# A decoder layer on one Trainium2 core: full-depth low K products and two gate projections moved ahead of waits

## The chip, the cores and the metric

The kernel runs on one core of one Trainium2 chip. The metric is device time in microseconds from start to end of one execution; lower is better. An execution that is profiled leaves a trace of each engine: PE (TensorE, matmuls) and PEld (its weight loads), DVE (VectorE), ACT (ScalarE), POOL (GpSimd), and the queue of SP (SyncE), which here issues nearly all DMA transfers.

## The reference, cut to what matters

One decoder layer in float32 over 1024 tokens of width 1024:

```python
u = x * (1.0 + scale_m) + shift_m
proj = u @ w_in                      # qa ka va | qb kb vb | ga gb
oa = sliding-window attention of 16 query heads on 2 K/V heads, with sinks
ob = dilated attention, 24 heads in 3 groups (dilation 1, 4, 16), merged by softmax of their log-sums
merged = sigmoid(ga) * (oa @ w_branch_a) + sigmoid(gb) * (ob @ w_branch_b)
x = layer_norm(ALPHA * x + (1.0 + gate_m) * (merged @ w_o))
u = x * (1.0 + scale_f) + shift_f
x = layer_norm(ALPHA * x + (1.0 + gate_f) * swiglu(u))
```

The products must have nearly float32 accuracy. TensorE multiplies values of a shorter format (`fp32r`), so each operand is kept as a high part (the rounded value, made by ACT) and a low part (the rest, made by a subtraction on DVE), and one product is three matmuls: high x high, high x low, low x high.

## The kernel before, in words

**First phase: projections and attention.** `w_in` is cut into 128-column chunks, in the order in which the attention uses them. One chunk is projected by `project`, which goes through `gemm_u`: 48 matmuls of 128x128 on 128x512 (two halves of the tokens, eight slices of the depth, three matmuls each), in 8 steps of 6. Work is grouped in 20 *units*. A B unit (12 of them, `p` pair of heads, `g` dilation group) needs three chunks, in the order K, V, Q; the first A unit needs Q, V, K, and the seven other A units only Q, as they share K and V. `stream` is a generator that yields after each of the 8 steps of each chunk, unit by unit. The first unit's three chunks and one chunk of gates are projected in the prologue (`early`), while the modulated input is still being made, so they yield nothing. Behind the last unit `stream` projects two more gate chunks, `tail_gates` (4 and 5 of `ga`), and stores them to the DRAM tile `ga_d`; the prologue's gate chunk (`early_gate_dc`, 3) is stored there too.

A loop over the units, in four quarters each (`subs`), issues the attention in turns with the stream: `scores` (PE), `turn_probs` of the quarter before (transposes on PE), `exponentials` (ACT), `weigh` of two quarters before (PE), and between them `pump`, which advances the stream to a given number of steps. `lengths` and `ends` hold how many steps belong to each unit; `LEAD` = 6 keeps the stream 6 steps ahead of the scores. Before the first scores the stream is pumped to `ends[0] + LEAD + 2` steps. `soon` and `tick` put off a function by a number of steps: the splitting of K and Q (`k_stacks`, `q_stacks`) is issued two or three steps after a chunk's end, somewhat later for the prologue's.

A unit has two heads, each of depth 64, on the lower (`LO`) and upper (`HI`) 64 partitions. `q_stacks` makes a tile of 128 partitions for each head: the high part of Q on the head's own half, the low part on the other half. `k_stacks` makes `kh`, with the high part of K on both halves (own half by ACT, line 448, other half by ACT again, line 449). So one matmul of depth 128 gives (Q high + Q low) x K high. The low part `kl` is made by DVE (line 454) on the own half; in a B unit both heads share one `kl` tile. The second product (line 501), Q high x K low, has a depth of 64: `LO` for one head, `HI` for the other. One call of `scores` issues four matmuls of depth 128 (line 495) and four of depth 64 (line 501).

**Second phase: branches.** The attention output is read back from DRAM (`oa_d`, `ob_d`), split into `o_hl` tiles by `o_parts` (lines 802, 117 and 118), and multiplied by the branch weights in 24 steps ("w" in `order`: three sets of 8 column chunks). Set 0 (first half of the A branch) has no gate of its own; in sets 1 and 2 each step's result is added up by DVE and multiplied by a gate tile `gt` (`merge`). The gates are in `order` as "g" entries, one ahead of each step of sets 1 and 2, but that of the first step of set 1 (gate 8) stands ahead of step 0. `make_gate` computes a gate with `gemm_u` or, for the indices in `made_early` (8 + the chunk's number), loads it from `ga_d`. `ada` is a generator of side work (the conditioning vectors), of which `make_gate` and the steps each take some.

The last attention outputs are finished while the second phase begins: the last pair's sums go to DRAM and back on POOL's queue, POOL scales the tile `o` and stores it to `oa_d` (lines 604, 609, 618, 619). Memory of the first phase's pool (`att`) is reused by the second phase's pools; a tile of the new pool waits for the last use of the old one at the same place. So where a tile of `att` lies decides what a tile of the second phase waits for.

**Weights.** `Weights` holds a list of pieces of 512 columns, in the order in which they are taken. Three raw tiles (`w_raw`) are loaded ahead on SP's queue; `step` splits the next piece (ACT line 78, DVE line 79) into one of four `w_hi`/`w_lo` pairs. Two steps of each projection and one of each branch step call it. All engines work off their instructions in the order in which the program issues them.

The second half of the kernel (`w_o`, the norm, the SwiGLU layer) is not touched.

Of the kernel before, what the change touches and what calls it, by code (L numbers as in the profile page):

```python
# [10 lines left out]
F32 = mybir.dt.float32  # L11
F32R = mybir.dt.float32r
I32 = mybir.dt.int32
AF = mybir.ActivationFunctionType
OP = mybir.AluOpType
# [3 lines left out]
P = 128  # L19
T = 1024  # L20
# [4 lines left out]
TH = T // 2  # L25
# [73 lines left out]
def decoder_layer(ctx: ExitStack, tc: tile.TileContext, I, out, dbg=None):  # L99
    nc = tc.nc  # L100
# [40 lines left out]

    ws = Weights(nc, wpool)
    EARLY = 3
    early_gate_dc = 3

    def add_chunk(src, pieces, kh, scale=None, dest=None):
        for i in range(pieces):
            ws.add(src[:, i * 512:(i + 1) * 512], kh, scale, dest)

    tail_gates = (4, 5)  # L150
    for e in range(EARLY, 46):
        add_chunk(I["w_in"][e], 2, 4)
    for dc in tail_gates:
        add_chunk(I["w_in"][46 + dc], 2, 4)
# [1 line left out]
    gate_of = {8 + dc: 46 + dc for dc in range(KC)}  # L156
    gate_of.update({16 + dc: 54 + dc for dc in range(KC)})
    branch_w = [I["w_branch_a"][0], I["w_branch_a"][1], I["w_branch_b"]]
    made_early = [8 + dc for dc in (early_gate_dc, *tail_gates)]
    order = []  # L160
    for i in range(len(steps)):
        g = 8 if i == 0 else i + 1
        if g in gate_of and i != 7:
            order.append(("g", g))
        order.append(("w", i))
    for kind, i in order:
        if kind == "g" and i not in made_early:
            add_chunk(I["w_in"][gate_of[i]], 2, 4)
        elif kind == "w":
            b, dc = steps[i]  # L170
            add_chunk(branch_w[b][dc], 1, 4)
# [268 lines left out]

        return rotary(e, r, then)

    def k_stacks(e, r, both, box):

        def stack(res, h):
            own, other = ((LO, HI), (HI, LO))[h]
            kh = att.tile([P, T], F32R, name="kh", bufs=4)
            nc.scalar.activation(kh[own], res[own], AF.Copy)
            nc.scalar.activation(kh[other], res[own], AF.Copy)
            box.setdefault("kh", []).append(kh)  # L450
            los = box.setdefault("kl", [])
            if both or not los:
                los.append(att.tile([P, T], F32R, name="kl", bufs=2))
            nc.vector.tensor_tensor(los[-1][own], res[own], kh[own], op=OP.subtract)  # L454
            if both:
                nc.vector.tensor_tensor(los[-1][other], res[own], kh[own], op=OP.subtract)
            elif h:
                los.append(los[0])

        def then(res):  # L460
            for h in range(2):
                soon(2 + h + (2 if e < EARLY else 0), lambda h=h: stack(res, h))

        return rotary(e, r, then)
# [20 lines left out]
    def scores(un, qr):  # L485

        box, prev, st = un["box"], un["prev"], un["st"]
        probs = att.tile([P, 2, 2, 2, P], F32, name="probs", bufs=2)
        un["probs", qr] = probs
        khs, kls = (box["kh"], box["kl"]) if "kv" not in un else ([kv_a["kh"][un["kv"]]] * 2, [kv_a["kl"][un["kv"]]] * 2)  # L490
        pss = [ps_s.tile([P, 2, 2, P], F32, name="s") for _ in range(2)]
        blocks = [(i, 2 * qr + i, 0 if prev(2 * qr + i) else 1) for i in range(2)]
        for i, b, lo in blocks:
            for h in range(2):
                nc.tensor.matmul(pss[h][:, i, lo:], box["q"][h][:, b * P:(b + 1) * P],  # L495
                                 khs[h][:, (b - 1 + lo) * P:(b + 1) * P], start=i == 0, stop=False,
                                 skip_group_check=True)

        for i, b, lo in blocks:
            for h, own in enumerate((LO, HI)):  # L500
                nc.tensor.matmul(pss[h][:, i, lo:], box["q"][h][own, b * P:(b + 1) * P],  # L501
                                 kls[h][own, (b - 1 + lo) * P:(b + 1) * P], start=False, stop=i == 1,
                                 skip_group_check=True)
        mx = att.tile([P, 2, 2], F32, name="mx", bufs=3)
        for h in range(2):
            for i, b, lo in blocks:
                nc.vector.tensor_tensor_reduce(  # L507
                    out=probs[:, h, i, lo:], in0=pss[h][:, i, lo:], in1=un["mask"][:, lo:], scale=QS, scalar=NEG,
                    op0=OP.add, op1=OP.max, accum_out=mx[:, h, i:i + 1])
            sl = slice(2 * qr, 2 * qr + 2)  # L510
            if "kv" in un:
                nc.vector.tensor_scalar(st[:, 0, h, sl], mx[:, h], un["sink"](h), -1.0, op0=OP.max, op1=OP.mult)  # L512
            else:
                nc.vector.tensor_scalar(st[:, 0, h, sl], mx[:, h], -1.0, None, op0=OP.mult)
# [159 lines left out]
    def sigmoid_half(dst, ps):  # L674
        nc.scalar.activation(dst, ps, AF.Tanh, scale=0.5)
        nc.vector.tensor_scalar(dst, dst, 0.5, 0.5, op0=OP.mult, op1=OP.add)

    def stream():
        for un in units:
            if "b" in un:  # L680
                p, g = un["b"]
                base, r = (p * 3 + g) * 3, B_DIL[g]
                yield from k_stacks(base, r, False, un["box"])
                yield from values(base + 1, r, un["box"])
                yield from q_stacks(base + 2, r, un["box"])
            else:
                yield from q_stacks(36 + un["a"] + 2 * (un["a"] > 0), 1, un["box"])
                if un["a"] == 0:
                    yield from values(37, 1, kv_a)
                    yield from k_stacks(38, 1, True, kv_a)  # L690
        for dc in tail_gates:
            g = att.tile([P, T], F32, name="r", bufs=1)
            yield from project(46 + dc, lambda t, ps: sigmoid_half(g[:, t * TH:(t + 1) * TH], ps))
            nc.sync.dma_start(ga_d[dc], g)

    lengths = [0 if n == 0 else 24 if "b" in un else 24 if un["a"] == 0 else 8 for n, un in enumerate(units)]
    ends = np.cumsum(lengths)
    total = ends[-1] + 8 * len(tail_gates)
    flow = stream()
# [37 lines left out]
    g_early = att.tile([P, T], F32, name="cst", bufs=1)  # L737
    for t, ps in enumerate(gate_banks):
        half = slice(t * TH, (t + 1) * TH)
        nc.scalar.activation(g_early[:, half], ps, AF.Tanh, scale=0.5)  # L740
        nc.scalar.activation(g_early[:, half], g_early[:, half], AF.Copy, bias=0.5, scale=0.5)
    nc.sync.dma_start(ga_d[early_gate_dc], g_early)
    pump(ends[0] + LEAD + 2)
    for s in range(len(subs) + 2):
# [104 lines left out]
    ada = ada_steps()  # L849
    gts = {}  # L850

    def make_gate(i, *steps):
        g = mix.tile([P, T], F32, name="gt", bufs=2)
        gts[i] = g
        if i in made_early:
            nc.sync.dma_start(g, ga_d[i - 8])
            return
        ps = [ps_2.tile([P, TH], F32, name="p2") for _ in range(2)]
        for n, t in enumerate(gemm_u(ps, ws.take(2), *steps)):
            if n % 4 == 2:  # L860
                next(ada, None)
            if t is not None:
                sigmoid_half(g[:, t * TH:(t + 1) * TH], ps[t])

    def merge(b, dc, t, ps, g):
        m = mrg(dc, t)
# [18 lines left out]
                    nc.sync.dma_start(dbg["mg"][dc * P:(dc + 1) * P, t * TH:(t + 1) * TH], mrg(dc, t))  # L885

    for kind, i in order:
        if kind == "g":
            if i in (8, 9, 17):
                ws.prepare(4)  # L890
# [328 lines left out]
    n = 0  # L1219
# [194 lines left out]
```

## Time and profile before

| | |
|---|---|
| median of 3 runs | 1885.06 us (1883.31 to 1887.6) |
| the profiled execution | 1886.68 us, of which its span 1884.6 us |
| mean granted clock of TensorE | 0.992 |
| PE busy | 1827.5 us, 8924 matmuls |
| DVE / ACT / POOL busy | 1154.8 / 784.0 / 600.0 us |
| bytes moved by DMA | 171.85 MB, mean 91 GB/s |

A row of the trace in order of time has the start in us from the span's start, the duration, engine, line, operation, output and inputs, the shapes, how many such instructions follow each other (x4), and in brackets how long the engine was idle before it and what ended that. Matmuls are pipelined: the next one starts before the one before has ended, so the distance of two starts tells what a matmul costs, not its duration. A row for a stretch ("A:B") gives its length, then the busy time of PE, PEld, DVE, ACT and POOL with their instructions, the granted clock, the share of time that the DMA engines were busy, and GB/s.

### The profile page before, as it was taken

Reading aid. Unit: us, or ns where it says so; the run is one execution under the profiler, and the core shown is the slowest. Engines: PE = TensorE matmul, PEld = TensorE weight load, DVE = VectorE, ACT = ScalarE, POOL = GpSimd, SP = SyncE. Lnnn points to the kernel's source line nnn. Section 1 sums busy time; section 2 is a strip of 40 time slices with the busy share of each in tenths; the row PEclk is TensorE's granted clock in tenths of the full one; section 3 lists DMA queues with packets and bytes.
Section 4 is the critical chain, followed back from the end, with each engine's and each line's share of the span. In section 5 each row is a group of like instructions: output and inputs, shape, how many; then the busy total and the mean of one; then the engine's idle time right before and its main releaser. Section 6 shows DMA issues by size and latency. Waiting matters only on the chain.

```text
span 1884.6 us, 24305 instructions
## 1 busy us (share of the span) xinstructions
PE 1827.5 (97%) x8924; PEld 1475.4 (78%) x8924; DVE 1154.8 (61%) x2136; ACT 784.0 (42%) x1664; POOL 600.0 (32%) x389
## 2 busy tenths in 40 slices
PE   6899999999999999989999999999999999999998
PEld 3678887877878767768888878878888888888886
DVE  5865567667667887643645365575565444674567
ACT  3544454544454667743112132653433333421122
POOL 2422323223223312100312242455664333531223
PEclk9999999999999999999999999999999999999999
DMA  8211112112111132144543223122222222442222
GB/s 280 91 34 35 35 36 79 40 39 76 42 57 63 41 95 76 57 168 155 208 137 137 79 72 134 57 90 101 85 78 85 89 79 89 151 134 71 97 84 89
DMA packets 72408, 171.85 MB, mean 91 GB/s; under 512 B 13089, under 2 KB 14177, under 8 KB 72290
## 3 DMA queue, kind: packets, MB, share of 16 engines
q1 hardware_dynamic: 71954, 169.26, 26.3%
q8 instruction: 70, 1.15, 0.3%
q0 software_dynamic: 336, 1.06, 0.2%
q14 instruction: 48, 0.39, 0.1%
HBM read 146.33 MB, written 23.95 MB: 90 GB/s over the span
## 4 chain that ended last, share of the span: by engine, by line
PE 81%; DVE 9%; ACT 4%; issue 3%; POOL 2%; DMA 1%; DVEq 0%; SPq 0%; POOLq 0%; ACTq 0%
PE pf L1108 22%; PE pj L137 7%; PE pj L139 7%; PE pj L138 6%; PE p L138 5%; PE p L139 5%; PE p L137 5%; PE pf L138 5%; PE pf L139 5%; PE pf L137 5%; PE pt L544 2%; PE po L567 2%; PE s L495 1%; PE s L501 1%; DVE probs L507 1%
## 5 line engine op out<-in xcount | busy, mean ns | idle before, releaser
L137 PE MATMUL pj<-u,w_hi 128*128 128x512 f32 x720 | 301.1, 418 | 0.0
L139 PE MATMUL pj<-u,w_lo 128*128 128x512 f32 x720 | 283.7, 394 | 0.0
L138 PE MATMUL pj<-u,w_hi 128*128 128x512 f32 x720 | 282.5, 392 | 0.0
L419 POOL TENSOR_TENSOR rb<-rb,sin_t 128x512 f32<-128x512 f32 x64 | 86.7, 1355 | 502.5 <-DVE rb L417 438.0
L118 DVE TENSOR_TENSOR w_lo<-r,w_hi 128x512 fp32r<-128x512 f32 x110 | 116.2, 1059 | 138.8 <-ACT w_hi L117 137.8
L79 DVE TENSOR_TENSOR w_lo<-w_raw,w_hi 128x512 fp32r<-128x512 f32 x148 | 131.2, 890 | 85.2 <-ACT w_hi L78 83.0
L522 ACT ACTIVATE probs<-probs,st 128x128 f32<-128x128 f32 (+1 forms) x320 | 146.0, 460 | 59.3 <-DVE st L512 30.1
L137 PEld LDWEIGHTS pj<-u,w_hi 128*128 128x128 f32 x720 | 136.2, 189 | 33.4 <-issue 4.7
L139 PEld LDWEIGHTS pj<-u,w_lo 128*128 128x128 f32 x720 | 135.8, 189 | 30.4
L138 PEld LDWEIGHTS pj<-u,w_hi 128*128 128x128 f32 x720 | 136.5, 190 | 22.4
L138 PE MATMUL pf<-wd,h 128*128 128x512 f32 x352 | 137.1, 389 | 0.0
L139 PE MATMUL pf<-wd,h 128*128 128x512 f32 x352 | 137.1, 389 | 0.0
L137 PE MATMUL pf<-wd,h 128*128 128x512 f32 x352 | 137.1, 389 | 0.0
L62 POOL TENSOR_TENSOR w_raw<-w_raw,gate 128x512 f32<-128x512 f32 x60 | 85.5, 1439 | 143.9 <-DMA w_raw<-in_w_down 120.6
L1327 DVE SCALAR_TENSOR_TENSOR zt<-zt,pf 128x512 f32<-128x512 f32 x112 | 75.3, 685 | 79.7 <-PE pf L139 79.7
L420 POOL TENSOR_TENSOR r<-ra,rb 128x512 f32<-128x512 f32 x63 | 114.5, 1817 | 6.1 <-DVE kl L454 1.3
L78 ACT ACTIVATE w_hi<-w_raw 128x512 fp32r<-128x512 f32 x148 | 90.8, 624 | 33.9 <-PE p L138 16.8
L546 ACT ACTIVATE ptsb<-pt 128x512 f32<-128x512 f32 (+1 forms) x128 | 63.5, 547 | 93.4 <-PE pt L544 93.0
L137 PE MATMUL p<-o_hl,w_hi 128*128 128x512 f32 x192 | 76.1, 396 | 6.8 <-ACT o_hl L117 6.8
L137 PE MATMUL p<-u,w_hi 128*128 128x512 f32 x208 | 82.2, 395 | 0.0
L139 PE MATMUL p<-u,w_lo 128*128 128x512 f32 x208 | 81.1, 390 | 0.0
L138 PE MATMUL p<-u,w_hi 128*128 128x512 f32 x208 | 81.0, 389 | 0.0
(305 smaller groups left out, 4266.8 us busy)
## 6 DMA issues: line engine op xcount, KB each, us to landing
w_raw<-in_w_in SPq DMA_DIRECT2D x116, 256.0 KB
r<-in_w_gate_up SPq DMA_DIRECT2D x47, 512.0 KB
a_raw<-in_w_ada SPq DMA_DIRECT2D x32, 512.0 KB
w_raw<-in_w_down SPq DMA_DIRECT2D x44, 256.0 KB
h_raw<-h_d SPq DMA_DIRECT2D x22, 512.0 KB
h_d<-g SPq DMA_DIRECT2D x40, 256.0 KB
wa<-in_w_ada_m SPq DMA_DIRECT2D x16, 512.0 KB
wb<-wt_d SPq DMA_DIRECT2D x24, 256.0 KB
```

The lines of the kernel that those rows point to most:

```text
L62: self.nc.gpsimd.tensor_tensor(self.raws[i], self.raws[i], scale(), op=OP.mult)
L78: self.nc.scalar.activation(hi, raw, AF.Copy)
L79: self.nc.vector.tensor_tensor(lo, raw, hi, op=OP.subtract)
L118: nc.vector.tensor_tensor(lo, src, hi, op=OP.subtract)
L137: nc.tensor.matmul(ps, w[0], m[0], start=first, stop=False)
L138: nc.tensor.matmul(ps, w[0], m[1], start=False, stop=False)
L139: nc.tensor.matmul(ps, w[1], m[0], start=False, stop=last)
L419: eng.tensor_tensor(b, b, sin_t[:, s], op=OP.mult)
L420: eng.tensor_tensor(residue_half(res, r, t), by_residue(a, r), by_residue(b, r), op=OP.add)
L522: nc.scalar.activation(pr, pr, AF.Exp, bias=st[:, 0, h, b:b + 1], accum_out=st[:, 1, h, b:b + 1])
L1108: nc.tensor.matmul(ps, w[:, c], m[:, k], start=first and k == 0 and n == 0, stop=k == 3 and n == 2, skip_group_check=True)
L1327: nc.vector.scalar_tensor_tensor(z, z, ALPHA if gi == 0 else 1.0, pd, op0=OP.mult, op1=OP.add)
```

## The change

Three things change.

1. *K stacks and scores.* The copy of K's high part to the other half is no longer made by ACT but by a DMA on SP's queue, inside the chip's memory. Each head has a `kl` tile of its own, with the low part on the own half (DVE) and copied to the other half by a second DMA. `kl` has four buffers of 4 KB in a partition instead of two. In `scores` the low product uses the whole Q tile and both halves of `kl`, so all eight matmuls have a depth of 128, and it now also holds Q low x K low. The two products of one block and head follow each other.
2. *A lead gate.* Chunk 6 of `ga` is projected in `stream` behind unit 0's chunks (which yield nothing), so ahead of unit 1's K chunk, and stored to `ga_d`. Its 8 steps count as unit 0's length, and the pump before the first scores runs to 16 steps instead of 8. Both operations of its sigmoid run on ACT (`act_sigmoid`). Its tile is a `wb` tile, which thereby gets its place in the pool earlier than before. In the second phase gate 14 is loaded.
3. *A bridge.* Gate 10 (chunk 2 of `ga`) is computed ahead of step 0, behind gate 8, and stored to `ga_d` (`kept=True`); it takes no side work from `ada`. At its own place in set 1 it is loaded.

The lists of weight pieces follow the new order.

```diff
-    early_gate_dc = 3
+    early_gate_dc, lead_gate_dc = 3, 6
...
-    for e in range(EARLY, 46):
+    for e in (46 + lead_gate_dc, *range(EARLY, 46)):
         add_chunk(I["w_in"][e], 2, 4)
...
-    made_early = [8 + dc for dc in (early_gate_dc, *tail_gates)]
+    made_early = [8 + dc for dc in (early_gate_dc, lead_gate_dc, *tail_gates)]
+    bridge = 10
...
+        if i == 0:
+            order.append(("b", bridge))
         order.append(("w", i))
     for kind, i in order:
-        if kind == "g" and i not in made_early:
+        if kind == "b" or (kind == "g" and i not in (*made_early, bridge)):
             add_chunk(I["w_in"][gate_of[i]], 2, 4)
...
-    def k_stacks(e, r, both, box):
+    def k_stacks(e, r, box):
         def stack(res, h):
             own, other = ((LO, HI), (HI, LO))[h]
             kh = att.tile([P, T], F32R, name="kh", bufs=4)
+            kl = att.tile([P, T], F32R, name="kl", bufs=4)
             nc.scalar.activation(kh[own], res[own], AF.Copy)
-            nc.scalar.activation(kh[other], res[own], AF.Copy)
+            nc.sync.dma_start(kh[other].bitcast(F32), kh[own].bitcast(F32))
+            nc.vector.tensor_tensor(kl[own], res[own], kh[own], op=OP.subtract)
+            nc.sync.dma_start(kl[other].bitcast(F32), kl[own].bitcast(F32))
             box.setdefault("kh", []).append(kh)
-            los = box.setdefault("kl", [])
-            if both or not los:
-                los.append(att.tile([P, T], F32R, name="kl", bufs=2))
-            nc.vector.tensor_tensor(los[-1][own], res[own], kh[own], op=OP.subtract)
-            if both:
-                nc.vector.tensor_tensor(los[-1][other], res[own], kh[own], op=OP.subtract)
-            elif h:
-                los.append(los[0])
+            box.setdefault("kl", []).append(kl)
...
             for h in range(2):
-                nc.tensor.matmul(pss[h][:, i, lo:], box["q"][h][:, b * P:(b + 1) * P],
-                                 khs[h][:, (b - 1 + lo) * P:(b + 1) * P], start=i == 0, stop=False,
-                                 skip_group_check=True)
-
-        for i, b, lo in blocks:
-            for h, own in enumerate((LO, HI)):
-                nc.tensor.matmul(pss[h][:, i, lo:], box["q"][h][own, b * P:(b + 1) * P],
-                                 kls[h][own, (b - 1 + lo) * P:(b + 1) * P], start=False, stop=i == 1,
-                                 skip_group_check=True)
+                for n, ks in enumerate((khs, kls)):
+                    nc.tensor.matmul(pss[h][:, i, lo:], box["q"][h][:, b * P:(b + 1) * P],
+                                     ks[h][:, (b - 1 + lo) * P:(b + 1) * P], start=i == 0 and n == 0,
+                                     stop=i == 1 and n == 1, skip_group_check=True)
...
+    def act_sigmoid(dst, ps):
+        nc.scalar.activation(dst, ps, AF.Tanh, scale=0.5)
+        nc.scalar.activation(dst, dst, AF.Copy, bias=0.5, scale=0.5)
...
+            if n == 0:
+                g = att.tile([P, T], F32, name="wb", bufs=1)
+                yield from project(46 + lead_gate_dc, lambda t, ps: act_sigmoid(g[:, t * TH:(t + 1) * TH], ps))
+                nc.sync.dma_start(ga_d[lead_gate_dc], g)
...
-    lengths = [0 if n == 0 else 24 if "b" in un else 24 if un["a"] == 0 else 8 for n, un in enumerate(units)]
+    lengths = [8 if n == 0 else 24 if "b" in un else 24 if un["a"] == 0 else 8 for n, un in enumerate(units)]
...
-    def make_gate(i, *steps):
+    def make_gate(i, *steps, kept=False):
         g = mix.tile([P, T], F32, name="gt", bufs=2)
         gts[i] = g
-        if i in made_early:
+        if i in (*made_early, bridge) and not kept:
             nc.sync.dma_start(g, ga_d[i - 8])
             return
         ps = [ps_2.tile([P, TH], F32, name="p2") for _ in range(2)]
         for n, t in enumerate(gemm_u(ps, ws.take(2), *steps)):
-            if n % 4 == 2:
+            if n % 4 == 2 and not kept:
                 next(ada, None)
...
+        if kept:
+            nc.sync.dma_start(ga_d[i - 8], g)
...
     for kind, i in order:
+        if kind == "b":
+            make_gate(i, kept=True)
+            continue
```

More of the change, by code (lines that the diff above doesn't have):

```diff
@@ L676, in sigmoid_half @@
         nc.vector.tensor_scalar(dst, dst, 0.5, 0.5, op0=OP.mult, op1=OP.add)
+    def act_sigmoid(dst, ps):
+        nc.scalar.activation(dst, ps, AF.Tanh, scale=0.5)
+        nc.scalar.activation(dst, dst, AF.Copy, bias=0.5, scale=0.5)
     def stream():
-        for un in units:
+        for n, un in enumerate(units):
             if "b" in un:
@@ L682, in stream @@
                 base, r = (p * 3 + g) * 3, B_DIL[g]
-                yield from k_stacks(base, r, False, un["box"])
+                yield from k_stacks(base, r, un["box"])
                 yield from values(base + 1, r, un["box"])
@@ L689, in stream @@
                     yield from values(37, 1, kv_a)
-                    yield from k_stacks(38, 1, True, kv_a)
+                    yield from k_stacks(38, 1, kv_a)
+            if n == 0:
+                g = att.tile([P, T], F32, name="wb", bufs=1)
+                yield from project(46 + lead_gate_dc, lambda t, ps: act_sigmoid(g[:, t * TH:(t + 1) * TH], ps))
+                nc.sync.dma_start(ga_d[lead_gate_dc], g)
         for dc in tail_gates:
@@ L739, in decoder_layer @@
         half = slice(t * TH, (t + 1) * TH)
-        nc.scalar.activation(g_early[:, half], ps, AF.Tanh, scale=0.5)
-        nc.scalar.activation(g_early[:, half], g_early[:, half], AF.Copy, bias=0.5, scale=0.5)
+        act_sigmoid(g_early[:, half], ps)
     nc.sync.dma_start(ga_d[early_gate_dc], g_early)
```

## The prediction

> **What bounds the kernel now.** I read the page first (busy shares, chain), then the waits of TensorE, then its order of time around each long wait. The page has PE busy nearly throughout, and the chain that sets the end is mostly PE:
>
> ```profile
> PE 1827.5 (97%) x8924; PEld 1475.4 (78%) x8924; DVE 1154.8 (61%) x2136; ACT 784.0 (42%) x1664; POOL 600.0 (32%) x389
> ...
> PE 81%; DVE 9%; ACT 4%; issue 3%; POOL 2%; DMA 1%; DVEq 0%; SPq 0%; POOLq 0%; ACTq 0%
> ```
>
> So the change can win only what PE loses: its idle time, the slow clock behind it, and dear matmuls. The waits of PE (who waited for whom, total, times, longest) say where:
>
> ```profile
> PE p L137 <- ACT o_hl L117: 6.8, 1, 6.8
> PE s L495 <- DVE qs L434: 5.8, 2, 5.0
> ...
> PE pt L474 <- ACT vt L478: 2.8, 3, 0.9
> PE pt L581 <- ACT ptsb L546: 2.6, 3, 0.9
> ```
>
> Each is touched by one part of the diff. The number of matmuls stays; two gate chunks change place. What one costs where PE is fed is seen in gate 8, 48 matmuls between these starts:
>
> ```profile
> 822.98 0.47 PE L137 MATMUL p<-u,w_hi 128*128 128x512 f32 x1
> ...
> 833.97 0.39 PE L137 MATMUL p<-o_hl,w_hi 128*128 128x512 f32 x1
> ```
>
> That is 10.99 us, 0.229 us a matmul: a row's 0.39 us is latency, and the pitch is what counts.
>
> **Part 1, the lead gate** (chunk 6 projected ahead of unit 1's K). PE's order of time at the first scores:
>
> ```profile
> 89.23 0.39 PE L139 MATMUL pj<-u,w_lo 128*128 128x512 f32 x1
> 94.59 0.44 PE L495 MATMUL s<-kh,qs 128*128 128x128 f32 x1 [4.97 <-DVE qs L434]
> 95.85 0.98 PE L495 MATMUL s<-kh,qs 128*128 128x128 f32 x3 [0.81 <-DVE qs L434]
> ...
> 97.48 0.79 PE L137 MATMUL pj<-u,w_hi 128*128 128x512 f32 x1
> ...
> 102.34 0.48 PE L139 MATMUL pj<-u,w_lo 128*128 128x512 f32 x1
> 102.66 0.39 PE L137 MATMUL pj<-u,w_hi 128*128 128x512 f32 x1
> ```
>
> Unit 1's K chunk ends at 89.46 (start plus pitch), the scores wait for the q stack, and the 12 projection matmuls from 97.48 run at 0.43 us instead of 0.23: a slow clock after idling. From 89.46 to 102.66 are 13.2 us, for work of 12 x 0.229 = 2.75 plus one call of scores, about 1.0: 9.4 us lost. The lead gate puts 10.99 us of PE work ahead, so the scores come up at about 100.4. Their last operand in the trace:
>
> ```profile
> 91.44 4.26 DVE L434 TENSOR_TENSOR qs<-o,qs 64x1024 fp32r<-64x1024 f32 x2
> ```
>
> It is ready at 95.70. Afterwards ACT has two tanh and two copies more in that stretch (1.2 us for each half, and the first waits for the gate's first half, about 2 us later than the K copy starts now), but two copies of K less, and VectorE no longer has unit 1's rotary between. So q is ready by 94 to 97, and the 5 us of slack also hide the four transfers of K halves. The same 48 matmuls go missing in the second phase, where PE is full, so they count nothing net. Gain 9.4; at worst, with the operands 3 us late and the clock slow again, 4.
>
> **Part 2, the bridge** (gate 10 ahead of the first branch product):
>
> ```profile
> 836.46 0.39 PE L139 MATMUL p<-o_hl,w_lo 128*128 128x512 f32 x1
> 843.65 0.80 PE L137 MATMUL p<-o_hl,w_hi 128*128 128x512 f32 x1 [6.80 <-ACT o_hl L117]
> ...
> 849.34 0.63 PE L139 MATMUL p<-o_hl,w_lo 128*128 128x512 f32 x1
> 849.76 0.52 PE L137 MATMUL p<-o_hl,w_hi 128*128 128x512 f32 x1
> ```
>
> Between 836.69 and 849.76 stand 12 matmuls, worth 2.75 us: 10.3 lost. What PE waits for is seen on POOL, ACT and DVE:
>
> ```profile
> 838.85 0.60 POOL L619 DMA_DIRECT2D oa_d<-o  x1 [0.30 <-POOL o L618]
> ```
>
> ```profile
> 842.54 2.00 ACT L117 ACTIVATE o_hl<-o_raw 128x1024 fp32r<-128x1024 f32 x2 [10.31 <-DMA oa_d<-o]
> 844.45 1.06 ACT L675 ACTIVATE gt<-p 128x512 f32<-128x512 f32 x2
> 845.40 0.63 ACT L78 ACTIVATE w_hi<-w_raw 128x512 fp32r<-128x512 f32 x1
> ```
>
> ```profile
> 843.63 2.36 DVE L118 TENSOR_TENSOR o_hl<-o_raw,o_hl 128x1024 fp32r<-128x1024 f32 x2 [10.15 <-ACT o_hl L117]
> 845.90 0.42 DVE L676 TENSOR_SCALAR gt<-gt 128x512 f32<-128x512 f32 x1
> 846.24 0.75 DVE L826 TENSOR_SCALAR acc<-a_raw,c_act 128x1024 f32<-128x1024 f32 x1
> ...
> 847.24 0.68 DVE L79 TENSOR_TENSOR w_lo<-w_raw,w_hi 128x512 fp32r<-128x512 f32 x1
> ```
>
> The third and fourth splits write memory that the last attention output still occupies, until its store lands at about 842.5. The bridge does not end that wait; it fills it: PE now works to 833.97 + 10.99 = 844.96. But what is queued behind it changes. The four pieces split ahead of time are now gate 8's and the bridge's, so the first product's own weights are split after the stalled o_hl, on the same ACT and DVE queues. As the K and wb tiles shift the pools (8 KB more of kl, wb earlier), I expect one split, not two, to wait: ACT 842.5 + 1.0, two tanh 1.0, w_hi 0.6 gives 845.1; DVE 843.6 + 1.2 + 0.4 + 0.7 + 0.4 + 0.7 gives w_lo at 847.0. The first two matmuls run at 845.1, the third needs w_lo: some 1.6 us idle. With both splits still waiting it is 2.6. Whether the clock then falls is bounded by two rows:
>
> ```profile
> 1198.64 0.66 PE L1036 MATMUL px<-ident,zt 128*128 128x128 f32 x4 [1.29 <-ACT raw L1037]
> ```
>
> ```profile
> 1235.96 0.80 PE L1108 MATMUL pf<-t3h,w_hi 128*128 128x512 f32 x1 [2.17 <-ACT w_hi L117]
> ```
>
> After 1.29 idle it stayed fast, after 2.17 it was slow (0.80 instead of 0.39), about 2.3 us dearer. [...] I take 10.3 - 1.6 = 8.7; ends 10.3 (no wait) and 3.5 (2.6 idle, slow clock, 2 us of later operands).
>
> **Part 3, low product over both halves.** Score calls: 20 units x 4 = 80, each 8 matmuls before and after. One 256-wide call (the first row is a stretch that holds its first two matmuls, the second its first three):
>
> ```profile
> 662.33 0.40 PE L495 MATMUL s<-kh,qs 128*128 128x256 f32 x2
> ```
>
> ```profile
> 662.33 0.52 PE L495 MATMUL s<-kh,qs 128*128 128x256 f32 x3
> ```
>
> ```profile
> 662.89 0.51 PE L501 MATMUL s<-kl,qs 64*128 64x256 f32 x4
> 663.33 1.09 PE L544 MATMUL pt<-ident,probs 128*128 128x128 f32 x8
> ```
>
> Full-depth matmuls follow at 0.52 - 0.40 = 0.12. Four of them take 0.56 up to the half-depth ones (662.33 to 662.89), so entering those costs 0.20 instead of 0.12; the four half-depth ones take 0.44. Now 1.00 a call; afterwards 8 x 0.12 = 0.96: -0.04 x 80 = -3 us. Bounds: 0.14 each (0.56/4), 1.12, +9.6; 0.11 each (0.44/4), 0.88, -9.6. I stay with the 0.12, which is the same kind of matmul. [...]
>
> ACT loses one K copy per half, 26 in all:
>
> ```profile
> 285.27 1.06 ACT L449 ACTIVATE kh<-r 64x1024 fp32r<-64x1024 f32 x1
> ```
>
> Two of these 1.06 us stand in ACT's queue ahead of each of the three vt and three ptsb evacuations that PE waits for (2.8 + 2.6 = 5.4 us). ACT is 2.1 us earlier there; the exponentials between them still wait for DVE's maxima, so I take 4.5, ends 0 and 5.4. Elsewhere ACT's relief hides behind PE.
>
> SP gets 52 transfers of 256 KB. In a B unit K is the first of three chunks and its scores come 20 projection steps later, tens of us. Behind a transfer that waits for ACT or DVE, SP holds weight pieces; but each of those waits for a DVE subtraction issued later still, and three lie ahead, so nothing. The tight place is the first A unit, whose K comes last:
>
> ```profile
> 622.41 1.22 DVE L454 TENSOR_TENSOR kl<-r,kh 64x1024 fp32r<-64x1024 f32 x1 [1.10 <-ACT kh L448]
> ```
>
> ```profile
> 627.93 0.62 PE L495 MATMUL s<-kh,qs 128*128 128x128 f32 x4
> ```
>
> ```profile
> oa_d<-o POOLq DMA_DIRECT2D x1, 512.0 KB, 3.6
> ```
>
> From 623.63 to 627.93 are 4.3 us; no row shows a transfer inside the chip's memory, the nearest is this store, 3.6 for twice the bytes. Wait 0 to 3, taken 0.5.
>
> **Reloads.** Gates 14 and 10 are loaded instead of computed in the second branch: five loading steps in a row instead of three. One such step now:
>
> ```profile
> 932.50:938.00 5.50, 5.50 (x26) 4.57 (x25) 4.18 (x4) 0.63 (x1) 3.62 (x3) 1.00 0.97 326
> ```
>
> DMA is full there (0.97, the next branch's inputs among it), yet PE stands at 5.50 of 5.50. A plain step of 5.5 us moves 0.25 + 0.5 + 0.5 MB, about 240 GB/s, under 326. Cost 0, up to 3 if weights fall behind.
>
> **Sum.** 9.4 + 8.7 + 3 + 4.5 - 0.5 = 25.1 us. The profiled execution took 1886.68 (span 1884.6), 1.6 above the median of 1885.06; it would become 1861.6, and the median 1860.0.
>
> **Rivals.**
> - The wait at the first product moves rather than goes: the new layout lets all four splits wait for the store at 842.5. Then ACT and DVE give w_lo about 3.5 us later, PE idles over 5 us and slows: 7 us less, 1867. For: the store's time does not change. Against: the first two splits do not wait now. 0.15.
> [...]
> - Slower: SP's order. If each of the 13 K stacks holds weights back until PE stands, it decides at 25.1/13 = 1.9 us a stack; at 3 us it gives 1899. For: every second transfer waits for DVE. Against: the slack above. 0.04.
> - The lead gate does not cover: K's halves come after 100.4, the first scores still idle and slow, 5 us lost, 1865. 0.06.
> - The five reloads starve the weights: 3 us, 1863. 0.04.
>
> **How the numbers follow.** My forecast has 0.66. The low end adds what the terms may bring more (1.6 + 6 + 0.9): 1851. The high end, with boundary, ACT and scores at their poor ends in part (14 lost): 1874. 0.2% is 3.8 us, about what a measurement of this kernel can tell from no change. Faster is the forecast and the first, fourth and fifth rivals, 0.91; within 0.2% the second, 0.05; slower 0.04.
>
> **What would show it.** No PE wait over 1 us at the first scores, and full clock around 100; 48 p2 matmuls ahead of the first o_hl product, and an idle under 2 us before or in it; scores as 8 matmuls of depth 128, 0.95 us a call; the vt and ptsb waits gone from PE's list. Wrong would be: a wait on a DMA of kh or kl, a slow stretch near 850, a call above 1.05.

## The result, and the profile after

The changed kernel takes 1867.28 us (median of 4 runs, 1866.08 to 1868.17), the kernel before, on the same chip, 1884.32 us (1883.31 to 1887.6). The ratio is 0.9906, 95% interval 0.9889 to 0.9923: 17 us faster, where 25 were forecast. (A second set of runs of both kernels, under e11_after, has 22 us.) The profiled execution took 1868.17 us, its span is 1866.1 us, 18.5 less than before.

The page after has PE busy 11.8 us less, ACT 24.0 us less (784.0 before), and in the chain that sets the end DMA now has 2% where it had 1%:

```profile
PE 1815.7 (97%) x8924; PEld 1479.6 (79%) x8924; DVE 1155.7 (62%) x2132; ACT 760.0 (41%) x1640; POOL 602.6 (32%) x389
...
PE 76%; DVE 11%; ACT 4%; issue 3%; DMA 2%; POOL 2%; SPq 0%; DVEq 0%; ACTq 0%; POOLq 0%
```

I cut the span where PE's order of time has the same matmul in both traces (start of the 13th projection matmul behind the first scores, of gate 8, of the first `w_o` product). Where a gate's 10.99 us moved from one stretch to another, that is taken out.

| stretch | before | after | gain | forecast |
|---|---|---|---|---|
| to the 13th matmul behind the first scores | 102.66 | 104.24, of it 10.99 moved in | 9.4 | 9.4 |
| attention, to gate 8 | 720.32 | 717.71 | 2.6 | 7.0 |
| second phase, to `w_o` | 289.85 | 272.36, with 10.99 moved out | 6.5 | 8.7 |
| the rest | 771.79 | 771.80 | 0 | 0 |

**The start** went as the prediction's rows said. PE's order of time after the change, no wait at the first scores and a pitch of 0.23 at once:

```profile
100.31 0.40 PE L139 MATMUL pj<-u,w_lo 128*128 128x512 f32 x1
100.55 0.22 PE L495 MATMUL s<-kh,qs 128*128 128x128 f32 x1
...
101.47 0.40 PE L137 MATMUL pj<-u,w_hi 128*128 128x512 f32 x1
101.71 0.39 PE L138 MATMUL pj<-u,w_hi 128*128 128x512 f32 x1
```

**The attention** lost what ACT's relief was to bring. The waits of PE (total, times, longest): the `ptsb` wait of line 581 is gone, `vt` is shorter, but two waits for DVE are new, for `v` and for the q stack.

```profile
PE s L495 <- DVE qs L437: 3.3, 3, 1.1
PE pt L538 <- DVE v L474: 2.8, 4, 0.9
...
PE pt L473 <- ACT vt L477: 1.9, 3, 0.7
```

What DVE itself waits for stands in DVE's waits, before first and then after: the load of the `wb` tile, 17.3 us instead of 5.2. Three of the four waits make up nearly all of it (6.1, 5.1 and 5.3 us).

```profile
DVE o L654 <- DMA wb<-wt_d: 5.2, 4, 1.8
```

```profile
DVE o L648 <- DMA wb<-wt_d: 17.3, 4, 6.1
```

At the first of the three, SP's queue (start, time on the queue, transfer) shows four K halves of 256 KB just ahead of `wb`, which DVE gets at 296.72 (row of its own):

```profile
285.14 0.47 SPq L453 DMA_DIRECT2D kh<-kh  x1
286.43 0.47 SPq L455 DMA_DIRECT2D kl<-kl  x1
287.00 0.53 SPq L55 DMA_DIRECT2D w_raw<-in_w_in  x1
287.63 0.59 SPq L453 DMA_DIRECT2D kh<-kh  x1
288.33 0.54 SPq L455 DMA_DIRECT2D kl<-kl  x1
288.92 0.71 SPq L603 DMA_DIRECT2D wb<-wt_d  x1
```

```profile
296.72 1.23 DVE L648 TENSOR_TENSOR o<-o,wb 128x1024 f32<-128x1024 f32 x1 [6.08 <-DMA wb<-wt_d]
```

Before the change only a weight load stood just ahead of it, and DVE waited 1.76 us:

```profile
287.74 0.36 SPq L55 DMA_DIRECT2D w_raw<-in_w_in  x1
288.14 1.15 SPq L609 DMA_DIRECT2D wb<-wt_d  x2
```

```profile
293.48 1.23 DVE L654 TENSOR_TENSOR o<-o,wb 128x1024 f32<-128x1024 f32 x1 [1.76 <-DMA wb<-wt_d]
```

After the change, the share of time that the DMA engines were busy (last but one number of each row) is at or near 1 from 288 to 294:

```profile
288.00:290.00 2.00, 2.00 (x20) 1.38 (x17) 1.90 (x12) 1.57 (x7) 0.00 (x0) 1.00 0.97 276
290.00:292.00 2.00, 1.38 (x9) 0.85 (x8) 0.64 (x2) 2.00 (x9) 0.00 (x0) 1.00 1.00 214
292.00:294.00 2.00, 2.00 (x15) 1.69 (x13) 0.00 (x0) 0.55 (x2) 0.00 (x0) 1.00 1.03 237
```

**The boundary** (from the first phase to the second). As forecast one split waits for the store; `w_hi` comes behind it on ACT, and PE idles twice:

```profile
842.10 1.06 ACT L117 ACTIVATE o_hl<-o_raw 128x1024 fp32r<-128x1024 f32 x1 [5.22 <-DMA oa_d<-o]
843.07 1.07 ACT L669 ACTIVATE gt<-p 128x512 f32<-128x512 f32 x2
844.02 0.63 ACT L78 ACTIVATE w_hi<-w_raw 128x512 fp32r<-128x512 f32 x1
```

```profile
843.61 0.39 PE L139 MATMUL p<-u,w_lo 128*128 128x512 f32 x1
844.70 0.50 PE L137 MATMUL p<-o_hl,w_hi 128*128 128x512 f32 x1 [0.70 <-ACT w_hi L78]
845.04 0.40 PE L138 MATMUL p<-o_hl,w_hi 128*128 128x512 f32 x1
846.41 0.50 PE L139 MATMUL p<-o_hl,w_lo 128*128 128x512 f32 x1 [0.97 <-DVE w_lo L79]
...
846.98 0.63 PE L138 MATMUL p<-o_hl,w_hi 128*128 128x512 f32 x1
...
850.39 0.39 PE L137 MATMUL p<-o_hl,w_hi 128*128 128x512 f32 x1
```

The eight matmuls from 846.98 to 850.39 run at 0.43 instead of 0.23, the slow clock: 1.6 us. From 843.84 (start plus pitch) to 850.39 stand 12 matmuls worth 2.75 us: 3.8 lost, 1.6 of it by the slow clock and 2.2 around the two idles. Before the change it was 10.3. The slow stretch near 850 is one of the prediction's own signs of being wrong; the other two, a wait for a K half's DMA and a score call above 1.05, did not come (the calls take 0.95).

### The profile page after: what moved, and what is told of

It is laid out like the page before. It is cut to its first block, busy times and chain, and to the rows that moved or that the text cites. A ratio compares the mean times of both kernels' runs of the same rounds, so it can differ in the third digit from the quotient of the medians.

```text
span 1866.1 us, 24418 instructions
## 1 busy us (share of the span) xinstructions
PE 1815.7 (97%) x8924; PEld 1479.6 (79%) x8924; DVE 1155.7 (62%) x2132; ACT 760.0 (41%) x1640; POOL 602.6 (32%) x389
## 4 chain that ended last, share of the span: by engine, by line
PE 76%; DVE 11%; ACT 4%; issue 3%; DMA 2%; POOL 2%; SPq 0%; DVEq 0%; ACTq 0%; POOLq 0%
PE pf L1114 21%; PE pj L137 6%; PE pj L139 6%; PE pj L138 6%; PE pf L138 5%; PE pf L137 5%; PE pf L139 5%; PE p L139 5%; PE p L138 5%; PE p L137 5%; PE s L495 2%; PE pt L538 2%; PE po L561 2%; DVE probs L501 1%; DMA wb<-wt_d 1%
## 5 line engine op out<-in xcount | busy, mean ns | idle before, releaser
L139 PE MATMUL pj<-u,w_lo 128*128 128x512 f32 x736 | 289.4, 393 | 0.0
L137 PEld LDWEIGHTS pj<-u,w_hi 128*128 128x128 f32 x736 | 138.7, 188 | 27.2 <-issue 4.1
L138 PEld LDWEIGHTS pj<-u,w_hi 128*128 128x128 f32 x736 | 138.8, 189 | 23.1
L495 PE MATMUL s<-kh,qs 128*128 128x256 f32 (+1 forms) x320 | 80.2, 284 | 7.4 <-DVE mx L501 4.1
L495 PE MATMUL s<-kl,qs 128*128 128x256 f32 (+1 forms) x320 | 79.8, 278 | 0.0
L436 ACT ACTIVATE qs<-r 64x1024 fp32r<-64x1024 f32 x38 | 40.1, 1055 | 94.4 <-POOL r L423 94.0
L137 PEld LDWEIGHTS pf<-wd,h 128*128 128x128 f32 x352 | 66.1, 188 | 13.8
```

The costliest lines, as they stand in the source:

```text
L137: nc.tensor.matmul(ps, w[0], m[0], start=first, stop=False)
L138: nc.tensor.matmul(ps, w[0], m[1], start=False, stop=False)
L139: nc.tensor.matmul(ps, w[1], m[0], start=False, stop=last)
```

## The experiments

My theories. T1: the K halves' bytes hold up the `wb` load, DVE stands, and what is queued behind it on DVE (the `v` copies, the q stack) reaches PE late. Rivals: T2, it is only SP's order (the `wb` issue comes later on that queue); T3, it is the engines' own work or the shift by the lead gate. For the boundary: what is left there are the splits queued behind the one that waits. All kernels here compute the whole layer. "Attention" and "second phase" are the stretches of the table above (the second as it is comparable with 289.85, a moved gate's 10.99 added back); the wait is DVE's for `wb<-wt_d`.

| kernel | median us | ratio to before, 95% | attention | second phase | wait for wb |
|---|---|---|---|---|---|
| before | 1884.3 to 1887.3 in four sets | | 720.3 | 289.9 | 5.2 |
| after | 1867.28 | 0.9906 (0.9889 to 0.9923) | 717.7 | 283.4 | 17.3 |
| e1_lead | 1878.33 | 0.996 (0.9948 to 0.9973) | 721.7 | 291.0 | 6.8 |
| e2_bridge | 1880.24 | 0.9973 (0.9964 to 0.9982) | 720.5 | 283.3 | 5.3 |
| e3_low | 1880.64 | 0.997 (0.9958 to 0.9981) | 714.9 | 288.9 | 14.9 |
| e4_engines | 1875.29 | 0.9946 (0.9933 to 0.9958) | 726.5 | 284.5 | 3.8 |
| e5_late | 1858.04 | 0.9849 (0.9834 to 0.9864) | 710.0 | 280.9 | 8.6 |
| e6_split | 1863.67 | 0.9882 (0.9865 to 0.9898) | 717.1 | 280.2 | 16.7 |
| e7_both | 1856.79 | 0.9843 (0.9828 to 0.9857) | 710.7 | 279.5 | 9.2 |
| e8_pool | 1869.71 | 0.991 (0.9896 to 0.9925) | 721.6 | 281.7 | 19.8 |
| e9_half | 1863.26 | 0.9873 (0.9858 to 0.9888) | 716.3 | 280.0 | 8.9 |
| e10_khact | 1862.26 | 0.9869 (0.9855 to 0.9884) | 716.3 | 279.5 | 6.6 |
| e11_after | 1865.25 | 0.9886 (0.9869 to 0.9902) | 718.1 | 281.9 | 17.6 |

### The three parts, each alone

**e1_lead** is the kernel before with the lead gate only (`early_gate_dc, lead_gate_dc = 3, 6`, the projection in `stream`, `lengths` 8 for unit 0).

> The kernel before with the lead gate alone. The stretch accounting of the two traces gives the start 9.4 us; attention and the boundary stay as they were before (the four splits, the gates 10 and 8 as before). Theory (the three parts add up): 1884.3 - 9.4 = about 1875, gate 8 starting 9.4 - 11.0 later and the rest equal. Rival (part of the 9.4 came from the earlier place of the K halves or of the wb tile in the pool): 3 us or more away from 1875. In the trace the vt and ptsb waits of PE stay near 2.8 and 2.6 us, and the wait of DVE for wb near 5 us in total.

7.5 us by the median, 6.8 by the span. The start brings its 9.4 again; two other places lose. One, 1.4 us, is in the attention, with a slow clock at a turn of the probabilities: from the eight transposes to the next matmul it takes 1.62 us, before the change 1.02 (677.05 to 678.07), and the matmuls behind run at 0.43. PE's longest wait for `mx` in this run is 1.1 us. PE's order of time:

```profile
679.62 1.97 PE L544 MATMUL pt<-ident,probs 128*128 128x128 f32 x8
681.24 0.78 PE L137 MATMUL pj<-u,w_hi 128*128 128x512 f32 x1
681.81 0.63 PE L138 MATMUL pj<-u,w_hi 128*128 128x512 f32 x1
682.24 0.63 PE L139 MATMUL pj<-u,w_lo 128*128 128x512 f32 x1
682.67 0.58 PE L137 MATMUL pj<-u,w_hi 128*128 128x512 f32 x1
```

At the same turn PE waited for `mx` 0.81 us before the change and 0.98 after it, and the projection matmuls behind ran at 0.23, so I take the slow clock for this execution's; that isn't shown. The other, 1.2 us, is in the second phase. The theory holds for the start; the total is 3.3 us off, which by the expectation would have spoken for the rival (1.5 of it is this set's kernel before, 1885.8). But the start gains its 9.4 with the K halves as they were, so no part of it needs them.

**e2_bridge** is the kernel before with the bridge only.

> The kernel before with the bridge alone, on the old layout of the pools, so that two splits of the attention output, not one, wait for the store that lands at about 842.5. Theory: the wait of PE at the first branch product is filled by gate 10, but the product's own splits come about 1 us later than in the changed kernel; 3.8 + 1 us of 10.3 stay, so the gain is 5 to 6: about 1879. Rival (the layout, not the bridge, brought the gain there): all of the wait stays, gain under 2.5 us. Other rival (a slow clock costs more once the single idle is over 2 us): gain 4 or less.

The median fell 5.6 us, as expected; the second phase gained 6.5, as much as in the changed kernel. Two splits do wait (ACT's row, `x2`), and PE's idles are longer, as expected, but no slow clock follows them:

```profile
842.79 2.01 ACT L117 ACTIVATE o_hl<-o_raw 128x1024 fp32r<-128x1024 f32 x2 [10.43 <-DMA oa_d<-o]
```

```profile
846.34 0.50 PE L137 MATMUL p<-o_hl,w_hi 128*128 128x512 f32 x1 [1.18 <-ACT w_hi L78]
846.68 0.39 PE L138 MATMUL p<-o_hl,w_hi 128*128 128x512 f32 x1
848.23 0.50 PE L139 MATMUL p<-o_hl,w_lo 128*128 128x512 f32 x1 [1.16 <-DVE w_lo L79]
```

The bridge, not the layout, brings the gain. That the slow clock came in the changed kernel after shorter idles (0.70 and 0.97) is taken up under e11 and at the end.

**e3_low** is the kernel before with the full-depth low product and the copies of K halves by DMA only.

> The kernel before with the full-depth low product and the copies of the K halves by DMA alone. By the traces the attention gained 2.6 us in the changed kernel: 3.5 from cheaper score calls less 0.9 of waits. Theory T1 (the transfers of the K halves crowd out the wb fetch at three places, DVE waits, its v copies and q stacks are late): DVE's wait for wb about 17 us in total as in the changed kernel, gain about 2.6, about 1882. Rival T3 (the waits of DVE and PE came from the lead gate's shift of eight steps, which put the units out of step with each other): DVE's wait for wb about 5 us as before, gain 6 to 7, about 1878. The boundary: four kl tiles shift the pools, so one split or two may wait; either way within 2 us of before.

DVE's wait for `wb` is 14.9 us without the lead gate and the bridge: T3's shift is out. The attention gained 5.4, twice the 2.6 of T1 and of the changed kernel: less of DVE's wait reached PE, whose wait for `v` is 1.3 us here and 2.8 in the changed kernel. The start was 1.8 shorter too, without the lead gate and behind the same 4.9 us idle: the 13th projection matmul starts at 100.82 instead of 102.66. A shorter slow clock is my estimate from these two starts. So the loss that the lead gate takes away was 7.6 to 9.4 us, by the execution.

### Bytes or order

**e4_engines**: the changed kernel with the other halves made by the engines again.

```diff
-            nc.sync.dma_start(kh[other].bitcast(F32), kh[own].bitcast(F32))
+            nc.scalar.activation(kh[other], res[own], AF.Copy)
...
-            nc.sync.dma_start(kl[other].bitcast(F32), kl[own].bitcast(F32))
+            nc.vector.tensor_tensor(kl[other], res[own], kh[own], op=OP.subtract)
```

> The changed kernel, but the other half of K's high and low part is made by the engines (ACT copies the high part as before, DVE subtracts the low part a second time) and no DMA copies them. T1 (transfers crowd out the wb fetch): DVE's wait for wb falls back to about 5 us, the score calls stay cheap (0.95), ACT's relief is gone and DVE has 26 subtractions of 1.2 us more, so the vt and ptsb waits return to their 5.4; attention about 3 us better than before, so the total lies within 2 us of the changed kernel's 1867. Rival T3 (the waits come from DVE's own order, not from the transfers): the wait for wb stays at about 17 us and the total is 3 to 6 us above the changed kernel.

The wait for `wb` is gone (3.8 us), as T1 says, but the expected total was wrong by 8 us. The `vt` wait alone is 8.2 us. Behind its longest idle, 1.89 us, PE has a slow clock (projection matmuls at 0.43 from 296.44 on), and the mean granted clock of the attention is 0.99 where it is 1.00 in the changed kernel:

```profile
PE pt L473 <- ACT vt L477: 8.2, 6, 1.9
...
PE pt L575 <- ACT ptsb L540: 3.6, 3, 1.2
```

So here both copies on the engines cost more than both by DMA (1875.29 against 1867.28), even where the DMA is in the way.

**e5_late**: the changed kernel with the same copies, issued four projection steps later.

```diff
+            def halves():
+                for x in (kh, kl):
+                    nc.sync.dma_start(x[other].bitcast(F32), x[own].bitcast(F32))
+            if e < EARLY or e == 38:
+                halves()
+            else:
+                soon(4, halves)
```

> The changed kernel with the two DMAs of each K half issued four projection steps later (not for the prologue's K and not for the first A unit's). The same bytes move, but no longer just ahead of the wb fetch. T1 (the K halves' transfers crowd out the wb fetch): DVE's wait for wb falls from 17.3 to about 5 us, the waits of PE for v and qs (2.8 and 3.3) go, ACT's relief shows, and the total falls by 3.5 to 4.5, to about 1863. T2 (SP's queue: the wb issue stands behind them): the same, as the order on SP changes too. T3 (neither; DVE's own work is late): wb wait as it is, total within 1 us of the changed kernel's 1867.

The wait fell by half (not to the 5 us expected), the `v` and `qs` waits left PE's list, and the kernel became 9.2 us faster than the changed one (7.2 by the second measurement of that, e11_after), where I expected 3.5 to 4.5; the attention alone gained 7.8. PE's busy time in the attention, second number of the rows (of the changed kernel, then of this one), leaves 14.6 us idle before and 8.1 now; the other 1.3 are busy time, by my estimate dearer matmuls behind such idles (the first behind an idle costs 0.34 instead of 0.23 in e2_bridge's rows). Another 2.4 us came at the boundary, where no slow clock followed the idle of 0.97.

```profile
104.24:821.95 717.71, 703.15 (x4057) 570.94 (x4056) 492.03 (x1258) 375.61 (x1020) 191.74 (x121) 1.00 0.26 74
```

```profile
104.05:814.01 709.96, 701.84 (x4058) 571.36 (x4056) 488.76 (x1258) 375.25 (x1020) 190.61 (x121) 1.00 0.27 74
```

DVE at the same place:

```profile
293.15 1.23 DVE L655 TENSOR_TENSOR o<-o,wb 128x1024 f32<-128x1024 f32 x1 [2.76 <-DMA wb<-wt_d]
```

T1 and T2 both allow this, since SP's order changed with it.

**e8_pool**: the changed kernel with the copies on POOL's queue, at the same places of the program (`nc.gpsimd.dma_start` for `nc.sync.dma_start`).

> The changed kernel with the two DMAs of each K half issued from POOL's queue instead of SP's, at the same places of the program. T1 (the bytes crowd out the wb fetch, whoever issues them): DVE's wait for wb stays over 10 us, total within 2 us of the changed kernel's 1867. T2 (on SP's queue the wb issue comes 0.8 us later behind the waiting issues of kh and kl): the wait for wb goes back to about 5 us and the total falls by 3 to 4. POOL's own work may get later behind issues that wait for ACT and DVE; that would show as new waits for POOL, up to some us slower.

This tells them apart. SP's queue now issues `wb` at 287.16, as early as in e5_late, where it was 287.17 (both rows below), and yet DVE gets it at 297.01, later than in the changed kernel:

```profile
287.16 1.45 SPq L603 DMA_DIRECT2D wb<-wt_d  x2
```

```profile
297.01 1.23 DVE L648 TENSOR_TENSOR o<-o,wb 128x1024 f32<-128x1024 f32 x1 [6.61 <-DMA wb<-wt_d]
```

```profile
287.17 1.12 SPq L610 DMA_DIRECT2D wb<-wt_d  x2
```

With the same issue time DVE gets the tile 3.9 us apart, by what else is in flight. So T2 alone falls and T1 holds: the early issue didn't help here while the copies' bytes were on their way. POOL issued the four of this place from 285.17 to 288.52, and from 286 to 288 the DMA engines were already busy 0.68 of the time (0.87 in the changed kernel, 0.08 in e5_late). The order still has a part in the changed kernel: there `wb` is issued 1.75 us later than in e5_late (288.92) and takes 7.80 us from issue to use instead of 5.98. The total, 1869.71, is 2.7 above 1867 where T1 allowed 2: PE's wait for `v` grew to 5.1, and a wait of 1.6 for a `kl` half is new.

### The boundary

**e6_split**: the changed kernel with the last of the four splits, the one that waits, issued behind the sixth step of the bridge.

```diff
-                parts = o_parts({8: 0, 9: 1, 17: 2}[i])
+                parts = o_parts({8: 0, 9: 1, 17: 2}[i], 3 if i == 8 else 4)
...
+            if kept and n == 5:
+                parts.extend(o_parts(0, 1))
```

> The changed kernel with the last of the four splits of the attention output, the one that waits for the store, issued behind the sixth step of the bridge, so that the splits of the first product's weights stand ahead of it on ACT and DVE. Theory (the 3.8 us left at the boundary are only the splits queued behind a waiting one, and the slow clock behind that): no idle of PE over 0.5 us and no slow matmuls at 845 to 850, gain 3.8, about 1863.5. Rival (the product needs that last split soon enough that the wait moves one product on): an idle of about 1 us some matmuls later and a slow clock again, gain 1 us or less.

As expected, 1863.67 us. The bridge runs into the first product without an idle and at full clock, and the second phase is 3.2 shorter (3.9 from gate 8's start to the 17th matmul of that product):

```profile
841.53 0.39 PE L139 MATMUL p<-u,w_lo 128*128 128x512 f32 x1
841.76 0.39 PE L137 MATMUL p<-o_hl,w_hi 128*128 128x512 f32 x1
841.99 0.39 PE L138 MATMUL p<-o_hl,w_hi 128*128 128x512 f32 x1
842.21 0.39 PE L139 MATMUL p<-o_hl,w_lo 128*128 128x512 f32 x1
```

**e7_both** has both edits.

> The changed kernel with both edits: K halves' DMAs four steps later, and the last split of the attention output behind the bridge's sixth step. Theory (two separate losses of 4.5 and 3.8): they add up, 1867.3 - 8.3 = about 1859. Rival (the boundary's state depends on where the units' tail stands): the sum of the two single gains is missed by more than 2 us.

1856.79 us, the fastest of all, 29.6 us below before. But it is only 1.25 us faster than e5_late, where 3.8 were expected of the second edit: in e5_late the product's two idles were 0.06 and 0.97 us, without a slow clock, so 2.4 of the 3.9 were already had. The rival was right here: the two single gains, 9.2 and 3.6, add up to 1854.4, 2.4 less than measured.

### The two gains, each taken back

**e9_half**: e7_both with the half-depth low product of before (its code in `scores`), and no copies of `kl` in the B units.

> The last version (K halves four steps later, last split moved; about 1856.8) with the half-depth low product of the kernel before and no copies of kl in the B units; kh is still copied by DMA. It isolates the depth of the low product. Theory (in the traces a half-depth call costs 2.9 us in itself over 80 calls, and the projection matmul right behind it 0.337 instead of 0.249, 51 times, 4.5 us more): +7.4, about 1864. The prediction's term (0.04 a call): +3, about 1860. Rival (the gain of the full depth is only that the engines have less to do): within 1.5 us of 1856.8.

6.5 us by the median (5.6 if each is taken from the kernel before of its own set, 1887.25 and 1886.37), 5.6 in the attention: nearer to 7.4 than to the prediction's 3. The rows show where the rest sits. Behind a half-depth call the first projection matmul costs 141.66 - 141.32 = 0.34 us, behind a full-depth one 101.71 - 101.47 = 0.24 (the start's rows above):

```profile
140.34 0.62 PE L501 MATMUL s<-kh,qs 128*128 128x128 f32 x4
140.89 0.50 PE L507 MATMUL s<-kl,qs 64*128 64x128 f32 x4
141.32 0.50 PE L137 MATMUL pj<-u,w_hi 128*128 128x512 f32 x1
141.66 0.39 PE L138 MATMUL pj<-u,w_hi 128*128 128x512 f32 x1
```

Summed over the distances of starts in the attention, the calls with their exits take 84.3 us in e9_half and 81.2 in e7_both (3.1), the projection matmuls that another follows 456.2 and 452.6 (3.6); 1.0 comes back, the turns of `vt` being earlier. The edit also puts back the order of the products, all of depth 128 first; no run tells order and depth apart.

**e10_khact**: e7_both with the other half of `kh` by ACT, as before the change.

> The last version (about 1856.8) with the high half of K copied by ACT as before, and only kl copied by DMA, four steps later. It isolates ACT's relief of 24 copies of 1.06 us. Theory (the vt waits, the st transposes behind ptsb and little else come back: 1.0 + 2.8): +3 to +4, about 1860.5. The prediction's term: +4.5, about 1861.3. Rival (the relief is hidden behind PE): within 1.5 us of 1856.8.

5.5 us by the median (4.6 from the kernels before of the two sets), 5.6 in the attention, more than the 3 to 4 that I expected. The waits that the prediction named come back:

```profile
PE pt L583 <- ACT ptsb L548: 3.7, 3, 1.3
PE pt L481 <- ACT vt L485: 3.0, 4, 0.9
```

The relief of ACT is worth 4.6 to 5.6 us once DVE isn't held up, at least what the prediction took for it (4.5).

**e11_after** is the changed kernel again.

> The changed kernel once more, to see what of its trace is the same in another execution: the wait for wb near 17 us, the vt, v and qs waits of PE, and the slow clock at the first branch product. [...] Rival (the slow clock follows from the idles alone): the eight slow matmuls again. Time 1867.3 within 2 us.

The wait for `wb` is 17.6 us, `v` 3.3 (2.8) and `qs` 2.2 (3.3): the waits belong to the kernel. The idles at the first product are there too, and this time, against the rival, no slow clock follows:

```profile
843.58 0.50 PE L137 MATMUL p<-o_hl,w_hi 128*128 128x512 f32 x1 [0.91 <-ACT w_hi L78]
843.91 0.40 PE L138 MATMUL p<-o_hl,w_hi 128*128 128x512 f32 x1
845.29 0.50 PE L139 MATMUL p<-o_hl,w_lo 128*128 128x512 f32 x1 [0.98 <-DVE w_lo L79]
```

It came instead in the attention, behind idles of 1.20 and 0.65 us in which PE waited for `v`, eight projection matmuls from 298.70 to 302.07. At the boundary idles of 0.70 and 0.97 had it behind them in one execution, 0.91 and 0.98 had not in the other; so its 1.6 us are no fixed part of the changed kernel's time. The median, 1865.25, is 2.0 us under the first one and 22.0 under the kernel before of its set, where the first set has 17.0: differences of a few us between sets can't be read as effects, and of the 2.7 us by which this span is shorter 1.7 stand at the 13th matmul already (102.57 instead of 104.24).

## Why the prediction was right in sign and range, and where its terms were wrong

- **Lead gate, 9.4: right**, in place and size (e1_lead gave it again). That the start behind the old idle varies by 1.8 us (e3_low, 100.82 instead of 102.66) was not seen.
- **Bridge, 8.7: right in mechanism, 2.2 too high.** One split waited and the product's weights came behind it, at 844.65 (`w_hi`) and 846.35 (`w_lo`) instead of the 845.1 and 847.0 worked out. The idles cost 2.2 instead of 1.6, as the split that waits for the store began only 0.4 us earlier than worked out (842.10), while PE was there 1.1 us earlier (843.84 instead of 844.96). The other 1.6 of the 2.2 by which the term was too high are the slow clock. The forecast took that for out of reach: it put the bound between idles of 1.29 and 2.17 us, each taken by itself, and two shorter ones, 0.70 and 0.97, had the slow clock behind them in one execution. e6_split shows that the whole rest, 3.9, was the queue behind one waiting split, with the slow clock that followed it in that execution.
- **Low product, 3: the mechanism right, the size half of it.** The call itself, which the prediction looked at, gives 2.9 to 3.1. The step that failed is that a call's cost was read from its first matmul to its last: the return to full depth is paid by the matmul *behind* the call, 0.34 instead of 0.24. e9_half puts the term at 5.6 to 6.5. The second rival (0.05, a time within 0.2%) is out: no run shows the full depth to cost time, and in a call of before the four half-depth matmuls take 0.44, 0.11 each, where one of full depth costs 0.12.
- **ACT's relief, 4.5: right in isolation (4.6 to 5.6 in e10_khact), but in the changed kernel it did not reach PE.**
- **SP's 52 transfers, "so nothing" but 0.5 at the first A unit: the step that failed.** The prediction asked whether a transfer could hold up SP's queue or PE's scores, and looked at the weights' load. It did not ask which other load is due at the same time and who stands behind it. In the trace of before the answer was there: the `wb` load was already waited for 5.2 us by DVE, with only a weight load just ahead of it. The price of copies at that moment is 7.8 us of attention in e5_late, and 6.4 between e6_split and e7_both, which differ in the same edit and were measured in one set. At the first A unit, where 0.5 was put down, PE waited for no copy.
- **Reloads, 0: right**; no wait of PE for them, and the second phase shows no other loss.

Attention as a sum: low product and relief together bring 10.4 in e5_late (720.3 to 710.0; the prediction had 7.5), the held-up `wb` takes 7.8 of it, and 2.6 are left. Two terms that were too low by 3 together hid part of the one that was missed, and the range took the rest. The high end of the range allowed 14 us of loss at boundary, ACT and scores, so it covered this by width and not by its reason: that the time fell inside it was in part luck. The rival that came nearest in time, all four splits waiting (1867), is not what happened.

## What to carry to other kernels

Before moving a copy from an engine to the DMA engines, list what else those engines fetch at that moment, and who waits in order behind each fetch: a copy with slack of its own can still cost by the load that it delays (7.8 us of attention here), and here moving the issue to another queue didn't help (1869.71), while moving it in time did (1858.04). Where an engine works off its instructions in the program's order, as ACT does here (`w_hi` at 844.02, behind a split that had waited 5.22 us), put a split or copy that must wait behind those that need not: 3.6 us in e6_split. Price a change of shape from the matmul ahead of the group to the second one behind it, and not from the group's own rows: here 5.6 to 6.5 us instead of 3.

## What was not expected of the hardware

- Half-depth matmuls cost at both ends: 0.20 us at the entry, where one of full depth costs 0.12 (prediction), and the first full-depth matmul of 512 columns behind them 0.34 instead of 0.24. The first matmul behind an idle costs the same 0.34 (844.70 to 845.04, and 846.34 to 846.68 in e2_bridge). What in the change of depth costs it is not shown.
- The slow clock came behind some idles and not behind others. At the boundary of the changed kernel it lasted from 846.98 to 850.39, 3.41 us, with a granted clock of 0.50, behind idles of 0.70 and 0.97 with two matmuls between them. In e1_lead one came in the attention, where no wait of PE is above 1.1. In e11_after 0.91 and 0.98 at the same place had none behind them, in e2_bridge 1.18 and 1.16 had none, and in the trace of before 1.29 had none and 2.17 had one (prediction). The long idles of before had it, too: the granted clock was 0.50 from 92.28 to 102.52, around the first scores (idle 4.97), and from 839.80 to 850.04, around the first branch product (6.80). How much idle it takes, and what else decides, stays open.
- DMA engines that were busy all the time didn't always move the same: the rows from 288 to 294 have 214 to 276 GB/s at 0.97 to 1.03, the prediction's row from 932.50 has 326 at 0.97. In e8_pool a load of 2 x 256 KB issued at 287.16 reached DVE's use of it only at 297.01.
